# Second layer's q, k and softmax weights turned by VectorE blocks and GpSimd transfers over DRAM, in place of TensorE transposes

## The chip, the cores and the metric

One core of a Trainium2 chip runs the whole program in one launch. The metric is the device time of one execution in microseconds (us). Three runs of the kernel before took 2663.75, 2664.67 and 2666.57 us; their median, 2664.67 us, is the time before. Weights arrive in the order in which the kernel reads them; laying them out so is done ahead of the launch and is not timed.

## The reference

Two layers of a bidirectional encoder over 256 tokens, width 2048, float32. A layer mixes tokens by two attentions in parallel, then applies a gated MLP with a depthwise convolution of width 3. Cut to what matters here:

```python
h = rmsnorm(x, norm_mix[l]) * (1 + sc_a) + sh_a
qa, ka, va, qb, kb, vb, ga, gb = split_cols(h @ w_in[l])
qa = rotary_partial(rmsnorm(qa, qn_a[l]), pos)      # 8 heads of 128; ka: 2 heads
ka = rotary_partial(rmsnorm(ka, kn_a[l]), pos)
ya = window_attention(qa, ka, va, sink_a[l]) @ w_proj_a[l]
qb, kb = rmsnorm(qb, qn_b[l]), rmsnorm(kb, kn_b[l])  # 8 heads of 128 each
yb = neighbourhood_attention(qb, kb, vb, rel_bias_b[l]) @ w_proj_b[l]
x = x + gt_a * ((sigmoid(ga) * ya + sigmoid(gb) * yb) @ w_out[l])
```

Each of the 16 heads of a layer computes softmax(q kT + bias or mask) v over 256 queries and 256 keys.

## The kernel before, in words

**Weights as a stream.** All weight blocks (128x128) of a layer stand in one order (`block_stream`, L90), cut into units of 16 blocks. For a unit, SyncE loads 1 MB into a tile of the pool `raw` (4 tiles, shared with the modulation rows `aw`, L225); ScalarE casts each half to its high part (`hl`, L297), VectorE subtracts to get the low part (L298), and TensorE multiplies both (`feature_block`, L314 to L316, three matmuls a block; `tokens`, L377 to L379, with 512 columns). The pool `hl` holds four halves, so the casts run at most two units ahead. What TensorE multiplies is written out by hand in that order: in the second layer 8 gate rows, nine groups of q, k and v (`QKV_GROUPS`, L33, four units each), the other gate rows, the projection of branch A (`ps<-oA`), the gates of branch B, the projection of branch B, the output, the MLP.

**Work between the units.** At the end of each unit `Stream.tick` (L331) runs `bg.tick` (L258): first what was deferred to the next unit (`bg.defer`, L246), then the jobs, each at a rate of steps a unit. After each group of q or k, `qk_rows` (L539) squares the rows on ScalarE (L547), takes the root as a power on GpSimd (L441), and three units later scales the rows into `qn` on VectorE (L556; one buffer). A unit later `turn` (L576) transposes `qn`, which has tokens on the partitions, head by head on TensorE against an identity matrix (L580), into PSUM, and ScalarE copies it out with the norm's gain (L581). Then `ready` lets heads start. The job `attention` (L842) advances every live head by one step and starts one more; its rate in the second layer is `ATT[1]` = 0.4 steps a unit in the q, k, v and gate stage and `ATT_B[1]` = 0.21 later. `attended(HA)` (L925) steps the job until the 8 heads of branch A are done, before the projection of A; `bg.finish(job)` (L952) does the rest before the projection of B.

**A head.** `head_a` or `head_b` (which loads its bias into `p` by SyncE, L825; `p` has two buffers) splits q and k into high and low parts. `attend` (L602): scores on TensorE (L607), maximum on VectorE (L610), exponential and scaling on ScalarE (L618, L626). In the next step four TensorE transposes turn `p` (L631) into the PSUM tile `tp`, and `split` (L389 ScalarE, L390 VectorE) writes high and low parts into `pT` (one buffer). In the next step TensorE multiplies v by `pT` (L639), and ScalarE and VectorE write `o` (L641, L642).

A tile scheduler puts each engine's instructions into one queue in order, by the program's order and by when it thinks operands are there; an engine never passes a waiting instruction. In the kernel before GpSimd issues no transfer; its work in the second layer's attention is the power at L441. The launch line (L1141) reserves 1024 bytes of each partition for descriptors of dynamic transfers.

Of the kernel before, what the change touches and what calls it, by code (L numbers as in the profile page):

```python
# [9 lines left out]
F32 = mybir.dt.float32  # L10
F32R = mybir.dt.float32r
# [4 lines left out]
P = 128  # L16
# [11 lines left out]
NEG = -1e30  # L28
SCALE = HEAD ** -0.5
GRID_W, NA_KH, NA_KW = 64, 8, 16  # L30


QKV_GROUPS = [1024, 0, 512, 2560, 3584, 1536, 3072, 4096, 2048]  # L33
# [44 lines left out]

H_RATE = [2.7, 1.7]

ATT = [1.288, 0.4]
ATT_B = [0.21, 0.21]

SCORES_3 = (1,)

ADA_ORDER = [[p * KC + k for k in range(KC) for p in ps] for ps in ((0, 1), (2,), (3, 4), (5,))]
ADA_ORDER = [i for part in ADA_ORDER for i in part]
# [47 lines left out]
def encoder(ctx: ExitStack, tc: tile.TileContext, a: dict, out: bass.AP):  # L135
# [16 lines left out]
    sm = pool("sm", 3)  # L152
    mm = pool("mm", 4, space=bass.MemoryType.PSUM)
    ax = pool("ax", 3, space=bass.MemoryType.PSUM)

    ident = const.tile([P, P], F32, name="ident")
    make_identity(nc, ident[:])
# [118 lines left out]
                pass  # L276

    bg = Paced()

    def unit_steps(l, u, by_halves=False):  # L280

# [254 lines left out]
            nc.vector.tensor_tensor(out=z[:], in0=ps[:, :S], in1=self.rbs[:], op=ALU.mult)  # L536
            return z, sh

    def qk_rows(pss, heads, rot, gain, dst, then):  # L539

        cols = 0
        n = heads * HEAD
        ss = sm.tile([P, 8], F32, name="qss", tag="qss")
        for t, ps in enumerate(pss):
            for i in range(heads):
                sq = at.tile([P, HEAD], F32, name="qsq", tag="qsq", bufs=1)
                nc.scalar.activation(  # L547
                    out=sq[:], in_=ps[:, cols + i * HEAD : cols + (i + 1) * HEAD], func=AF.Square,
                    accum_out=ss[:, t * heads + i : t * heads + i + 1],
                )  # L550
        rs = sm.tile([P, 8], F32, name="qrs", tag="qrs")
        rsqrt(rs[:, : 2 * heads], ss[:, : 2 * heads], HEAD, 2 * heads)
        def norm():
            qn = at.tile([P, 2, 4, HEAD], F32, name="qn", tag="qn", bufs=1)
            for t, ps in enumerate(pss):
                nc.vector.tensor_tensor(  # L556
                    out=qn[:, t, :heads],
                    in0=ps[:, cols : cols + n].rearrange("p (h d) -> p h d", d=HEAD),
                    in1=rs[:, t * heads : (t + 1) * heads].unsqueeze(2).broadcast_to([P, heads, HEAD]),
                    op=ALU.mult,  # L560
                )
            if rot is not None:
                x1, x2 = qn[:, :, :heads, :HALF], qn[:, :, :heads, HALF:ROT]
                tab = [rot[:, i].unsqueeze(2).broadcast_to([P, 2, heads, HALF]) for i in range(4)]
                tm = []
                for i in range(2):
                    z = ev.tile([P, S], F32, name=f"rt{i}", tag="z")
                    z = z[:].rearrange("p (i t h d) -> p i t h d", i=2, t=2, h=4)
                    tm += [z[:, 0, :, :heads], z[:, 1, :, :heads]]
                for i, src in enumerate((x1, x2, x2, x1)):  # L570
                    nc.vector.tensor_tensor(out=tm[i], in0=src, in1=tab[i], op=ALU.mult)
                nc.vector.tensor_tensor(out=x1, in0=tm[0], in1=tm[1], op=ALU.subtract)
                nc.vector.tensor_tensor(out=x2, in0=tm[2], in1=tm[3], op=ALU.add)
            bg.defer(lambda: turn(qn))

        def turn(qn):  # L576
            for t in range(2):
                ps = ax.tile([P, 4, P], F32, name="qtp", tag="ax")
                for h in range(heads):
                    nc.tensor.transpose(ps[:, h], qn[:, t, h], ident[:])  # L580
                nc.scalar.activation(  # L581
                    out=dst[:, :, t * P : (t + 1) * P], in_=ps[:, :heads], func=AF.Identity, scale=gain
                )
            then()

        bg.defer(lambda: bg.defer(lambda: bg.defer(norm)))
# [12 lines left out]

        return ((0, 0), (0, 1), (1, 0))[: 2 * len(x) - 1]  # L600

    def attend(q, k, v, p, mask, scale, sink, o):  # L602

        sc = ax.tile([P, 2, S], F32, name="sc", tag="ax")
        for t in range(2):
            for i, j in by(q):
                nc.tensor.matmul(sc[:, t], q[i][:, t * P : (t + 1) * P], k[j], start=i + j == 0, stop=(i, j) == by(q)[-1])  # L607
        m = sm.tile([P, 2], F32, name="m", tag="m")
        for t in range(2):
            nc.vector.tensor_tensor_reduce(  # L610
                out=p[:, t], in0=sc[:, t], in1=mask[:, t], scale=scale, scalar=-3.0e38 if sink is None else sink,
                op0=ALU.add, op1=ALU.max, accum_out=m[:, t : t + 1],
            )
        nm = sm.tile([P, 2], F32, name="nm", tag="nm")
        nc.vector.tensor_scalar(out=nm[:], in0=m[:], scalar1=-1.0, scalar2=None, op0=ALU.mult)
        den = sm.tile([P, 2], F32, name="den", tag="den")
        for t in range(2):
            nc.scalar.activation(out=p[:, t], in_=p[:, t], func=AF.Exp, bias=nm[:, t : t + 1], accum_out=den[:, t : t + 1])  # L618
        if sink is not None:
            es = sm.tile([P, 2], F32, name="es", tag="es")  # L620
            nc.scalar.activation(out=es[:], in_=nm[:], func=AF.Exp, bias=sink)
            nc.vector.tensor_tensor(out=den[:], in0=den[:], in1=es[:], op=ALU.add)
        ri = sm.tile([P, 2], F32, name="ri", tag="ri")
        nc.vector.reciprocal(out=ri[:], in_=den[:])
        for t in range(2):
            nc.scalar.activation(out=p[:, t], in_=p[:, t], func=AF.Copy, scale=ri[:, t : t + 1])  # L626
        yield
        tp = ax.tile([P, 2, S], F32, name="tp", tag="ax")
        for k in range(2):
            for t in range(2):  # L630
                nc.tensor.transpose(tp[:, k, t * P : (t + 1) * P], p[:, t, k * P : (k + 1) * P], ident[:])  # L631
        pT = at.tile([P, 2, 2, S], F32R, name="pT", tag="pT", bufs=1)
        split(pT, tp[:])
        v = v()
        yield
        po = ax.tile([P, 512], F32, name="po", tag="ax")
        for i, j in by(v):
            for b in range(2):
                nc.tensor.matmul(po[:, :S], v[i][:, b], pT[:, j, b], start=i + j + b == 0, stop=i + b == 2)  # L639
        o = o()  # L640
        nc.scalar.copy(o[:, 0], po[:, :S])  # L641
        nc.vector.tensor_tensor(out=o[:, 1], in0=po[:, :S], in1=o[:, 0].bitcast(F32), op=ALU.subtract)  # L642
# [115 lines left out]
    for l in range(L):  # L758
# [41 lines left out]
        def head_a(i):  # L800
            g = i // (HA // GA)
            if i >= 6:
                oA.append(paired(F32R, f"oA{l}_{i}"))
            elif i % 2 == 0:
                o = place(("y0", "y1", "y2")[i // 2], 4, F32R, f"oA{l}_{i}")
                oA.extend((o[:, :2], o[:, 2:]))
            q = in_halves(qTa[:, i], f"qA{l}_{i}", "qh", l in SCORES_3)
            if i % (HA // GA) == 0:
                kvs[0] = in_halves(kTa[:, g], f"kA{l}_{g}", "kh", l in SCORES_3)
            k = kvs[0]  # L810
            yield
            p = at.tile([P, 2, S], F32, name="p", tag="p")

            def v():
                if i % (HA // GA) == 0:
                    kvs[1] = in_halves(packs[0][:, 1:4:2, g * HEAD : (g + 1) * HEAD], f"vA{l}_{g}", "vh", True)
                return kvs[1]

            yield from attend(q, k, v, p, tables[0], SCALE, sink[:, i : i + 1], lambda: oA[i])

        def head_b(hb):
            b, i = packs[1 + hb // 4], hb % 4
            v = b[:, 4:8].rearrange("p (t a) s -> p t (a s)", t=2)
            p = at.tile([P, 2, S], F32, name="p", tag="p")
            nc.sync.dma_start(p[:], a["bias"][l, hb])  # L825
            q = in_halves(b[:, 8 + i], f"qB{l}_{hb}", "qh", l in SCORES_3)
            k = in_halves(b[:, i], f"kB{l}_{hb}", "kh", l in SCORES_3)
            yield
            yield from attend(
                q, k, lambda: in_halves(v[:, :, i * HEAD : (i + 1) * HEAD], f"vB{l}_{hb}", "vh", True), p, p, 1.0, None,  # L830
                lambda: oB_of(hb),
            )

        def oB_of(hb):
# [36 lines left out]
        for pi, (groups, gates) in enumerate(parts):  # L871
            last = pi == len(parts) - 1
            for g, part in enumerate(groups):
# [21 lines left out]
                    for t in range(2):  # L895
                        nc.scalar.copy(rows[:, t, vcol:], pss[t][:, vcol:])
                if g == 0:
                    qk_rows(pss, GA, rots[1], gains[:, 1:2], kTa, turned)
                elif g < 3:
                    qk_rows(pss, 4, rots[0], gains[:, 0:1], dst, turned)  # L900
                elif vcol is None:
                    qk_rows(pss, 4, None, gains[:, 3:4] if g in (3, 6) else gains[:, 2:3], dst, turned)
                else:
                    turned()
                if g == 2:
# [243 lines left out]
```

## Time and profile before

| what | value |
|---|---|
| three runs | 2663.75, 2664.67, 2666.57 us |
| profiled execution | span 2663.2 us from its first to its last instruction (no other time of this execution is listed) |
| TensorE (PE) busy | 2650.9 us, 100% of the span |
| VectorE (DVE) busy | 2102.2 us, 79% |
| ScalarE (ACT) busy | 1412.8 us, 53% |
| GpSimd (POOL) busy | 36.2 us, 1% |
| bytes moved | 700.41 MB in 102039 packets |

Times in the trace count from the start of the span. The second layer's attention lies from 1438 us (the first q or k transpose) to 1802 us (the last gate of branch B); the projection of A begins at 1658 us. A row of the timeline gives the start, the length, engine, line, operation, output and inputs, and in brackets how long the engine had been idle and what it waited for. A row of the groups gives the count, busy time and mean length of one instruction. TensorE's matmuls are pipelined: the length of one (390 ns with 512 columns) is longer than the distance between two (227 ns), so its busy time is no measure of what a removed matmul saves; the distance in the timeline or the chain of work is.

### The profile page before, as it was taken

The page shows a single profiled execution, that of the slowest core. Times are in us where ns is not written, and L with a number is a line of the kernel's source. Part 1 is how long each engine was busy: PE and PEld are TensorE (multiplying, and loading weights), DVE is VectorE, ACT ScalarE, POOL GpSimd, SP SyncE. Part 2 cuts the span into 40 slices and gives each one's busy share as a digit, 9 for nine tenths or more (in the row PEclk, how much of TensorE's full clock was granted, in tenths as well). Part 3 has the DMA queues.
Part 4 walks back from the last instruction along what each step waited for, and adds up shares of the span by engine and source line. Part 5 has one row for each costly group of instructions (what it writes and reads, how often), then busy time and mean ns, then how long its engine had stood idle before and what let it go on. Part 6 is the DMA issues. An engine that isn't in the chain of part 4 may idle for free.

```text
span 2663.2 us, 50845 instructions
## 1 busy us (share of the span) xinstructions
PE 2650.9 (100%) x21256; PEld 2565.7 (96%) x21256; DVE 2102.2 (79%) x2959; ACT 1412.8 (53%) x2284; POOL 36.2 (1%) x25
## 2 busy tenths in 40 slices
PE   9999999999999999999999999999999999999999
PEld 7888899999999999999998889999999999999999
DVE  8898998997987888788976667768888866655664
ACT  5445865456644555355555566554565445544553
POOL 0001100000000000000000000000000000000000
PEclk9999999999999999999999999999999999999999
DMA  9987789885787878788766666666747765555554
GB/s 372 351 327 292 262 300 352 317 320 199 291 294 287 302 288 295 289 294 289 290 217 254 228 229 231 245 252 253 285 173 288 297 256 190 190 194 194 197 191 143
DMA packets 102039, 700.41 MB, mean 263 GB/s; under 512 B 12721, under 2 KB 15025, under 8 KB 17969
## 3 DMA queue, kind: packets, MB, share of 16 engines
q1 hardware_dynamic: 101810, 697.17, 71.4%
q8 instruction: 166, 2.72, 0.4%
q14 instruction: 63, 0.52, 0.1%
HBM read 695.03 MB, written 2.10 MB: 262 GB/s over the span
## 4 chain that ended last, share of the span: by engine, by line
PE 89%; DVE 6%; ACT 1%; issue 1%; DMA 1%; POOL 0%; SPq 0%; DVEq 0%; ACTq 0%
PE ps L314 25%; PE ps L316 25%; PE ps L315 25%; PE ps_t L377 4%; PE ps_t L379 4%; PE ps_t L378 4%; DVE hl L298 2%; DVE aw L226 2%; DMA aw<-in_aw 1%; PE sc L607 1%; PE po L639 1%; ACT hl L297 1%; PE tp L631 1%; POOL qrs L441 0%; PE qtp L580 0%
## 5 line engine op out<-in xcount | busy, mean ns | idle before, releaser
L298 DVE TENSOR_TENSOR hl<-w,hl 128x1024 fp32r<-128x1024 f32 x928 | 1128.3, 1222 | 360.0 <-ACT hl L297 357.6
L297 ACT CAST hl<-w 128x1024 fp32r<-128x1024 f32 x928 | 970.7, 1049 | 748.5 <-PE ps L316 518.1
L314 PE MATMUL ps<-h,hl 128*128 128x256 f32 x3328 | 922.8, 277 | 1.3 <-DVE ya L915 0.6
L315 PE MATMUL ps<-h,hl 128*128 128x256 f32 x3328 | 919.8, 276 | 0.0
L316 PE MATMUL ps<-h,hl 128*128 128x256 f32 x3328 | 919.8, 277 | 0.0
L314 PEld LDWEIGHTS ps<-h,hl 128*128 128x128 f32 x3328 | 624.8, 188 | 2.4 <-DVE ya L915 0.8
L315 PEld LDWEIGHTS ps<-h,hl 128*128 128x128 f32 x3328 | 625.3, 188 | 0.4 <-DVE h L470 0.2
L316 PEld LDWEIGHTS ps<-h,hl 128*128 128x128 f32 x3328 | 624.4, 188 | 0.0
L226 DVE CUSTOM_DVE_ANT_0 aw<-aw,cact,ab 128x2048 f32<-128x2048 f32 x189 | 443.5, 2347 | 48.8 <-DMA aw<-in_aw 47.8
L377 PE MATMUL ps_t<-hl,h 128*128 128x512 f32 x576 | 223.1, 392 | 2.6 <-ACT h L469 2.1
L378 PE MATMUL ps_t<-hl,h 128*128 128x512 f32 x576 | 224.9, 391 | 0.3
L379 PE MATMUL ps_t<-hl,h 128*128 128x512 f32 x576 | 224.3, 390 | 0.0
L994 DVE SCALAR_TENSOR_TENSOR u<-ps,cw,u 128x255 f32<-128x255 f32 x304 | 146.1, 481 | 66.5 <-ACT u L992 62.2
L992 ACT ACTIVATE u<-ps,cw 128x256 f32<-128x256 f32 x152 | 85.9, 565 | 187.9 <-PE ps L316 187.5
L316 PE MATMUL ps<-merged,hl 128*128 128x256 f32 x512 | 141.8, 277 | 0.4 <-DVE hl L298 0.4
L315 PE MATMUL ps<-merged,hl 128*128 128x256 f32 x512 | 141.6, 277 | 0.0
L314 PE MATMUL ps<-merged,hl 128*128 128x256 f32 x512 | 141.6, 277 | 0.0
L315 PE MATMUL ps<-act_o,hl 128*128 128x256 f32 x512 | 141.4, 276 | 0.0
L316 PE MATMUL ps<-act_o,hl 128*128 128x256 f32 x512 | 141.3, 276 | 0.0
L314 PE MATMUL ps<-act_o,hl 128*128 128x256 f32 x512 | 141.2, 276 | 0.0
L377 PEld LDWEIGHTS ps_t<-hl,h 128*128 128x128 f32 x576 | 107.9, 188 | 26.1 <-ACT h L469 3.1
L378 PEld LDWEIGHTS ps_t<-hl,h 128*128 128x128 f32 x576 | 108.1, 188 | 23.7 <-DVE hl L298 1.9
(231 smaller groups left out, 4612.5 us busy)
## 6 DMA issues: line engine op xcount, KB each, us to landing
w<-in_ws SPq DMA_DIRECT2D x463, 1024.0 KB, 4.9
aw<-in_aw SPq DMA_DIRECT2D x189, 1024.0 KB, 6.1
p<-in_bias SPq DMA_DIRECT2D x16, 256.0 KB, 4.2
x<-in_xT SPq DMA_DIRECT2D x4, 512.0 KB, 5.3
aw_o<-in_aw SPq DMA_DIRECT2D x2, 1024.0 KB, 12.3
out<-x SPq DMA_DIRECT2D x16, 128.0 KB, 2.1
w<-in_ws SPq DMA_DIRECT2D x2, 512.0 KB, 11.7
aw_b<-in_aw SPq DMA_DIRECT2D x1, 1024.0 KB, 18.1
```

Of the source, the lines that this page charges most:

```text
L226: nc.vector.tensor_tensor_reduce(out=raw[:], in0=raw[:], in1=cact[:], scale=1.0, scalar=ab[:, i : i + 1], op0=ALU.mult, op1=ALU.add, accum ...
L297: nc.scalar.copy(hl[:, 0], r)
L298: nc.vector.tensor_tensor(out=hl[:, 1], in0=r, in1=hl[:, 0].bitcast(F32), op=ALU.subtract)
L314: nc.tensor.matmul(out, hi, act[0], start=first, stop=False)
L315: nc.tensor.matmul(ps[:, :S], hi, act[1], start=False, stop=False)
L316: nc.tensor.matmul(out, lo, act[0], start=False, stop=last)
L377: nc.tensor.matmul(ps[:], xh, hi, start=kc == kcs[0], stop=False)
L378: nc.tensor.matmul(ps[:], xh, lo, start=False, stop=False)
L379: nc.tensor.matmul(ps[:], xl, hi, start=False, stop=kc == kcs[-1])
L607: nc.tensor.matmul(sc[:, t], q[i][:, t * P : (t + 1) * P], k[j], start=i + j == 0, stop=(i, j) == by(q)[-1])
L992: nc.scalar.activation(out=u, in_=ps, func=AF.Identity, scale=w[:, 1:2], bias=w[:, 3:4])
L994: nc.vector.scalar_tensor_tensor(out=u[:, to], in0=ps[:, of], scalar=w[:, j : j + 1], in1=u[:, to], op0=ALU.mult, op1=ALU.add)
```

## The change

In the second layer (`MOVED = (1,)`) no transpose runs on TensorE. VectorE turns each 32x32 block of the tile in place (`blocks`). Then GpSimd issues eight transfers (`scatter`), each from 32 partitions of one half of the tokens, which put the blocks into their transposed places in a DRAM tile; one contiguous piece is 32 floats, 128 bytes. A transfer of a full q or k group has 512 such pieces, one of `p` or of the first group (2 heads) has 256. A further transfer reads the DRAM tile back: for q and k straight into its place (`dst`), where ScalarE then applies the gain in place; for `p` two transfers, each into a tile of its own (`pk`, pool `ev`, tag `r`, two buffers), from which `split` writes `pT` in two parts. Blocks, scatter, read-back and gain are a unit apart (`in_turn`). A head of the second layer has two more steps, in which it only waits, and the rates rise from 0.4 to 0.5 and from 0.21 to 0.32.

```diff
+BLOCK = 32
-ATT = [1.288, 0.4]
-ATT_B = [0.21, 0.21]
+ATT = [1.288, 0.5]
+ATT_B = [0.21, 0.32]
+MOVED = (1,)
+    dram = pool("dram", 2, space=bass.MemoryType.DRAM)
+    def once(fn):
+        due = [fn]
+        def run():
+            if due:
+                due.pop()()
+        return run
+    def in_turn(*fns):
+        def run(i):
+            fns[i]()
+            if i + 1 < len(fns):
+                bg.defer(lambda: run(i + 1))
+        bg.defer(lambda: run(0))
+    def blocks(t):
+        nc.vector.transpose(out=t, in_=t)
+    def scatter(y, rows):
+        to = y[:].rearrange("(b i) n (t a j) -> t a i n b j", i=BLOCK, t=2, a=P // BLOCK)
+        for t, row in enumerate(rows):
+            src = row.rearrange("p n (b j) -> p n b j", j=BLOCK)
+            for a in range(P // BLOCK):
+                nc.gpsimd.dma_start(to[t, a], src[a * BLOCK : (a + 1) * BLOCK])
...
-    def qk_rows(pss, heads, rot, gain, dst, then):
+    def qk_rows(pss, heads, rot, gain, dst, then, moved=False):
...
         def turn(qn):
+            if moved:
+                for t in range(2):
+                    blocks(qn[:, t, :heads].rearrange("p h d -> p (h d)"))
+                y = dram.tile([P, heads, S], F32, name="qY", tag="qY")
+                def scaled():
+                    nc.scalar.activation(out=dst, in_=dst, func=AF.Identity, scale=gain)
+                    then()
+                in_turn(
+                    lambda: scatter(y, [qn[:, t, :heads] for t in range(2)]), lambda: nc.gpsimd.dma_start(dst, y[:]), scaled
+                )
+                return
...
-    def attend(q, k, v, p, mask, scale, sink, o):
+    def attend(q, k, v, p, mask, scale, sink, o, moved=False):
...
         yield
+        if moved:
+            blocks(p[:].rearrange("p t k -> p (t k)"))
+            y = dram.tile([P, 2, S], F32, name="pY", tag="pY")
+            turned = []
+            def back():
+                for k in range(2):
+                    turned.append(ev.tile([P, S], F32, name="pk", tag="r", bufs=2))
+                    nc.gpsimd.dma_start(turned[k][:], y[:, k])
+            steps = [once(lambda: scatter(y, [p[:, t].rearrange("p (k s) -> p k s", k=2) for t in range(2)])), once(back)]
+            in_turn(*steps)
+            yield
+            yield
+            for step in steps:
+                step()
+            pT = at.tile([P, 2, 2, S], F32R, name="pT", tag="pT", bufs=1)
+            for k in range(2):
+                split(pT[:, :, k], turned[k][:])
+        else:
...
+            split(pT, tp[:])
```

The calls of `attend` and `qk_rows` pass `l in MOVED`.

More of the change, by code (lines that the diff above doesn't have):

```diff
@@ L627, in attend @@
         yield
[L628 to L633, printed above, removed]
+        if moved:
[16 more added lines that the diff above has]
+        else:
+            tp = ax.tile([P, 2, S], F32, name="tp", tag="ax")
+            for k in range(2):
+                for t in range(2):
+                    nc.tensor.transpose(tp[:, k, t * P : (t + 1) * P], p[:, t, k * P : (k + 1) * P], ident[:])
+            pT = at.tile([P, 2, 2, S], F32R, name="pT", tag="pT", bufs=1)
+            split(pT, tp[:])
         v = v()
@@ L817, in v @@
                 return kvs[1]
-            yield from attend(q, k, v, p, tables[0], SCALE, sink[:, i : i + 1], lambda: oA[i])
+            yield from attend(q, k, v, p, tables[0], SCALE, sink[:, i : i + 1], lambda: oA[i], l in MOVED)
         def head_b(hb):
@@ L830, in head_b @@
                 q, k, lambda: in_halves(v[:, :, i * HEAD : (i + 1) * HEAD], f"vB{l}_{hb}", "vh", True), p, p, 1.0, None,
-                lambda: oB_of(hb),
+                lambda: oB_of(hb), l in MOVED,
             )
@@ L897, in encoder @@
                 if g == 0:
-                    qk_rows(pss, GA, rots[1], gains[:, 1:2], kTa, turned)
+                    qk_rows(pss, GA, rots[1], gains[:, 1:2], kTa, turned, l in MOVED)
                 elif g < 3:
-                    qk_rows(pss, 4, rots[0], gains[:, 0:1], dst, turned)
+                    qk_rows(pss, 4, rots[0], gains[:, 0:1], dst, turned, l in MOVED)
                 elif vcol is None:
-                    qk_rows(pss, 4, None, gains[:, 3:4] if g in (3, 6) else gains[:, 2:3], dst, turned)
+                    qk_rows(pss, 4, None, gains[:, 3:4] if g in (3, 6) else gains[:, 2:3], dst, turned, l in MOVED)
                 else:
```

## The prediction

> **What bounds the kernel now.** I read the page's busy times first, then the busy time by stretches, then the chain of work over the second layer's attention, then the timeline around it.
>
> ```profile
> PE 2650.9 (100%) x21256; PEld 2565.7 (96%) x21256; DVE 2102.2 (79%) x2959; ACT 1412.8 (53%) x2284; POOL 36.2 (1%) x25
> ...
> PEclk9999999999999999999999999999999999999999
> ```
>
> TensorE is never idle and its clock is granted in full, so a matmul taken out of its queue is time gained, and every wait that reaches it is time lost. The stretches of the stage that changes (before and after 1647 us, where the last head of branch A must be done):
>
> ```profile
> core 0: us, PE busy (x) PEld busy (x) DVE busy (x) ACT busy (x) POOL busy (x), PEclk, DMA share, GB/s
> 1440.00:1647.00 207.00, 206.94 (x1149) 179.85 (x1148) 142.09 (x221) 126.75 (x279) 9.87 (x6) 1.00 0.63 233
> 1647.00:1802.00 155.00, 155.00 (x1361) 155.00 (x1360) 107.56 (x169) 83.32 (x150) 0.00 (x0) 1.00 0.67 246
> ```
>
> VectorE works 142 of 207 us, ScalarE 127, the 16 DMA engines 63%, GpSimd 10. There is room everywhere but on TensorE. How much lead the others have over it shows in the timeline:
>
> ```profile
> 1433.24 1.05 ACT L297 CAST hl<-w 128x1024 fp32r<-128x1024 f32 x1 [1.67 <-PE ps_t L379]
> 1435.96 1.05 ACT L297 CAST hl<-w 128x1024 fp32r<-128x1024 f32 x1 [1.67 <-PE ps_t L379]
> 1437.04 1.23 DVE L298 TENSOR_TENSOR hl<-w,hl 128x1024 fp32r<-128x1024 f32 x1 [1.50 <-ACT hl L297]
> ```
>
> TensorE uses half a unit in 1435.96 - 1433.24 = 2.72 us, a unit in 5.44. A cast starts when one of four half buffers comes free, so three halves are ready: 3 x 2.72 = 8.2 us, less 1.05 and 1.23 to make the next, leaves a **lead of 5.9 us**. ScalarE or VectorE may stand still that long before TensorE waits.
>
> **The change, part by part: the gain.** 52 transposes of q and k (2 heads x 2, six groups of 4 x 2) and 64 of `p` (16 x 4) go; the built program of the changed kernel has exactly 116 fewer. The chain has their price:
>
> ```profile
> 1438.64 0.44 PE qtp L580 x4
> 1460.92 0.87 PE qtp L580 x8
> ...
> 1518.85 0.44 PE tp L631 x4
> ```
>
> 0.44 / 4 = 0.87 / 8 = 0.11 us each, so 116 x 0.11 = 12.8 us at most; the timeline shows 0.35 us for four where the next matmuls close up (0.09 each):
>
> ```profile
> 1600.78 0.60 PE L631 MATMUL tp<-ident,p 128*128 128x128 f32 x4
> 1601.13 0.94 PE L607 MATMUL sc<-kA,qA 128*128 128x256 f32 x6
> ```
>
> That gives 10.2 us. I take **12 us**.
>
> **VectorE and ScalarE.** Every price is from these rows of the attention's stretch:
>
> ```profile
> L390 DVE TENSOR_TENSOR pT<-tp,pT 128x512 fp32r<-128x512 f32 x16 | 10.9, 682 | 0.1
> L389 ACT CAST pT<-tp 128x512 fp32r<-128x512 f32 x16 | 9.5, 595 | 0.0
> L389 ACT CAST vB<-packB 128x256 fp32r<-128x256 f32 x8 | 3.4, 421 | 0.0
> L390 DVE TENSOR_TENSOR vB<-packB,vB 128x256 fp32r<-128x256 f32 x8 | 3.3, 415 | 0.0
> L581 ACT ACTIVATE packB<-qtp,gains 128x512 f32<-128x512 f32 x8 | 5.1, 687 | 0.0
> ```
>
> No block transpose is in the trace; nearest is 682 ns for 512 columns (one input instead of two may make it half, a slower form double): 28 x 0.68 + 2 x 0.42 = 20 us, 10 to 40. The split of `p` in two costs VectorE 32 x 0.415 - 10.9 = 2.4 us more, ScalarE 32 x 0.421 - 9.5 = 4.0. ScalarE's gain over 1024 columns (some 1.05 us, as the cast of that width) in place of two of 0.69 saves under 3 us. In the first stretch (14 blocks of q and k, 8 of heads, some 15 us) VectorE rises to 157 of 207 us and is still idle a quarter of it; the added work comes in pieces of 0.7 us, inside a lead of 5.9. Cost **0**, hidden behind TensorE's matmuls; were the lead gone, the 20 + 2.4 = 22 us would be paid.
>
> **The transfers.** GpSimd's queue gets 7 x 8 scatters of q and k, 16 x 8 of `p`, 7 + 32 read-backs: 223 transfers; the scatters are 48 x 512 + 8 x 256 + 128 x 256 = 59,392 pieces of 128 bytes. The trace has no transfer of GpSimd's. What it has:
>
> ```profile
> q1 hardware_dynamic: 101810, 697.17, 71.4%
> ...
> out<-x SPq DMA_DIRECT2D x16, 128.0 KB, 2.1
> ...
> ab<-in_ab SPq DMA_DIRECT2D x2, 48.0 KB, 6.2
> ...
> gains<-in_gains SPq DMA_DIRECT2D x2, 2.0 KB, 4.4
> ```
>
> ```profile
> 1435.57 0.33 SPq L225 DMA_DIRECT2D aw<-in_aw  x1
> ```
>
> Below, one transfer costs the queue what SyncE needs to issue one, 0.33 us, and the rest overlaps; above, each waits for the one ahead to land, 6.2 us (`ab`, 128 short rows under load). The nearest row is `out<-x`: also into DRAM, 128 rows, 2.1 us. A scatter of 512 pieces has four times the pieces and half the bytes; I put it between 2.1 and the 4.4 of `gains` (128 rows of 16 bytes), at **3.0 us**; one of 256 pieces, of which the built order lets several be under way, between 0.33 and 2.1, at **1.3**; a read-back at 1.0. [...]
>
> **Who waits.** The scatter starts when VectorE has made the blocks. Two units and the gain's unit later, 16.3 us after them, ScalarE meets the gain; behind it stand the casts of `hl`. With the lead that is 22 us for 8 x 3.0 = 24, a landing of 2.1, the read-back's 1.0 and its 2.1: 29. It is 7 us late by itself. Behind the scatter in GpSimd's queue stands the next group's power (L441), VectorE's `qn` waits for that and the subtractions stand behind `qn`; already now:
>
> ```profile
> DVE qn L556 <- POOL qrs L441: 10.6, 6, 1.8
> ```
>
> It is the same lateness, paid once. For `p`, four units (21.8 us) and the lead stand against 8 x 1.3 + 2.1 + 2 + 2.1 = 16.6: in time, unless a group's scatter is ahead in the queue. From the fourth group on it is, as the built order mixes them. SyncE's load of `p` for a head of branch B must wait until the scatter two heads back has read its buffer, and the weight loads stand behind it. Now it waits for the transposes:
>
> ```profile
> SPq L825 <- PE tp L631: 35.7, 14, 5.2
> ```
>
> Eight scatters land 12.5 us after the blocks, and the built order puts that load some two units (10.9 us) after them: 1.6 us, inside the raw tiles' lead. Cost 0; with a backlog it is not.
>
> **The sum.** As each wait pushes the next, I count GpSimd's queue as a whole up to the last head of branch A, whose turned weights the projection of A needs. In the built order six full groups, the small one and eight heads stand ahead of it: 48 x 3.0 + 8 x 1.3 + 6 x 1.0 + 64 x 1.3 + 16 x 1.0 = 259.6 us, and 9.9 of powers (the stretch's POOL column), and 3 us for landing and split: 272.5 against 207 us. **65.5 us late.** In the second stretch eight heads take 8 x (8 x 1.3 + 2) = 99 of 155 us: nothing. So 2663.2 - 12 + 65.5 = 2716.7 us for the profiled execution's span; the median of the three runs, 2664.67, lies 1.5 above that span: **2718 us**.
>
> **The rivals.**
>
> A. *The transfers are hidden.* If 512 pieces cost 1.8 and 256 cost 0.95 or less (the queue overlaps landings), with 0.6 a read-back, the demand is 86 + 8 + 61 + 13 + 10 = 178 of 204 us, and a lone group takes 14.4 + 4.8 = 19 of 22 us. Then only the gain is left: 2664.7 - 12 = 2653 (2651.9 with 12.8). For it: GpSimd is idle and a third of the DMA time is free. Against it: 59,392 pieces where the whole kernel now has 102,039 packets. It ends on the other side, and decides where the queue's demand falls below the stretch. Chance 0.21. If it misses by as much as it gains, no change: 0.05.
>
> B. *Every scatter waits for the one ahead.* At 4.4 us (`gains`) for 512 and 2.1 (`out<-x`) for 256: 211 + 17 + 6 + 134 + 16 + 10 + 3 = 397, 190 late: 2664.7 - 12 + 190 = 2843. For it: eight transfers to a group, one queue, and a reserve of 1024 bytes for descriptors. Against: landing times under SyncE's 1 MB loads contain the wait behind those in one queue. [...] Chance 0.20.
>
> C. *The pieces crowd the weights.* In the first stretch 48 x 512 + 8 x 256 + 64 x 256 = 43,008 pieces are 2688 on each engine; 37% of 207 us is free, 77 us, so it decides from 28 ns a piece. The q1 row gives 0.714 x 16 x 2663.2 / 101,810 = 0.30 us for a packet of 6.8 KB; by bytes alone 128 take 6 ns. At 50 ns, 134 us: 57 late, 2710. It would show as ScalarE's casts waiting for `w`. Chance 0.10.
>
> D. *VectorE keeps GpSimd out.* If each of the 142 transfers of the first stretch also waited for a subtraction (1.23 us, above): 175 more, 2893. [...] The trace of before has no transfer of GpSimd's and cannot show it.
>
> For D: VectorE is busy two thirds of the stretch. Against: the 10 us that GpSimd's powers took in it show no such delay, 1.6 us each. Chance 0.05.
>
> That the change does not do what it says is excluded by the built program's count of transposes.
>
> **How the numbers follow.** Forecast 2718 us, chance 0.39; A 0.21, no change 0.05, B 0.20, C 0.10, D 0.05. Faster by over 0.2% (below 2659.3): A alone, 0.21. Slower by over 0.2% (above 2670.0): 0.39 + 0.20 + 0.10 + 0.05 = 0.74. 0.2% is about what a measurement of this kernel can tell from no change. The range: below, A's full gain, 2651; above, prices that reach past B's 2843 to D's 2893. It leaves out the bound of 6.2 us a transfer (142 x 6.2 alone is 880 us, far over 207) and the halves of D above 2893.
>
> **What would show it.** Right: `qtp` and `tp` gone from the second layer; TensorE idle between 1440 us and the projection of A by some 60 us, put down to VectorE's `qn` and ScalarE's gain, which wait for GpSimd and its transfers; the stretch after it as long as before less its transposes; a full group's eight scatters holding GpSimd's queue for some 24 us. Wrong: no idle TensorE (A); casts of `hl` waiting for `w` from DRAM (C); a stretch of the first layer or the MLP that changes its length, which no step here touches; a scatter that occupies the queue for over 4 us (B).

## The result and the profile after

The changed kernel takes **2775.59 us** (median of 4 runs, 2774.72 to 2780.65) against 2664.6 us of the kernel before (4 runs, 2663.75 to 2666.57): 1.042 times as long, interval 1.040 to 1.043. The forecast was 2718 us: the sign and the place were right, the loss of 111 us is twice the 53 foreseen. The profiled execution took 2776.42 us, its span is 2774.2.

The page of the changed kernel; the busy times, then TensorE's share, the granted clock in 40 slices of 69.4 us, and GpSimd's DMA queue (packets, MB, share of the DMA engines):

```profile
PE 2666.5 (96%) x21140; PEld 2571.6 (93%) x21140; DVE 2115.8 (76%) x3005; ACT 1409.0 (51%) x2293; POOL 178.7 (6%) x248
...
PE   9999999999999999999997877799999999999999
...
PEclk9999999999999999999998888899999999999999
...
q0 software_dynamic: 8368, 15.22, 2.2%
```

All is as before but for the slices of the second layer's attention: there TensorE idles, and its clock, always full before, is granted at eight tenths. The same stretch of work by windows, first the kernel before, then the changed one (from 1440 us to the first matmul of the projection of A, and on to that of B; the columns are the stretch, its length, the busy time of PE, PEld, DVE, ACT and POOL, the granted clock, the DMA share and GB/s):

```profile
1440.00:1658.00 218.00, 217.94 (x1245) 190.85 (x1244) 149.57 (x235) 133.43 (x292) 9.87 (x6) 1.00 0.63 232
1658.00:1802.30 144.30, 144.30 (x1267) 144.30 (x1266) 100.08 (x154) 76.94 (x136) 0.00 (x0) 1.00 0.68 249
```

```profile
1440.00:1764.50 324.50, 233.51 (x1171) 197.49 (x1170) 161.11 (x269) 132.74 (x300) 108.11 (x156) 0.85 0.57 188
1764.50:1913.80 149.30, 144.89 (x1225) 144.30 (x1225) 105.17 (x166) 79.55 (x143) 39.20 (x65) 0.97 0.74 267
```

The first stretch is 106.5 us longer, the second 5. TensorE stood still for 324.5 + 149.3 - 233.5 - 144.9 = **95.4 us**. Its matmuls were busy for 378.4 us where before they took 362.2 and should have taken about 352 without the transposes (9.9 us, measured below): **26 us** more, at a clock of 0.85. 95.4 + 26.1 - 9.9 = 111.6, the whole difference. The one group of matmuls below shows the slower clock: in the stretch up to 1764 us the mean of one (in ns, behind the comma), before and after:

```profile
L378 PE MATMUL ps_t<-hl,h 128*128 128x512 f32 x223 | 86.9, 390 | 0.0
```

```profile
L413 PE MATMUL ps_t<-hl,h 128*128 128x512 f32 x222 | 93.3, 420 | 43.8 <-DVE hl L333 43.5
```

Who waited for what in the changed kernel from 1416 to 1830 us (total us, times, longest):

```profile
POOL qY L313 <- issue: 129.1, 45, 6.7
...
ACT packB L618 <- DMA packB<-qY: 67.2, 4, 26.0
DVE qn L591 <- POOL qrs L476: 62.4, 6, 21.2
POOL pY L313 <- issue: 60.4, 46, 4.1
...
ACT packA L618 <- DMA packA<-qY: 46.7, 3, 19.1
ACT pT L424 <- DMA pk<-pY: 44.1, 13, 11.9
```

These are the waits the prediction named: ScalarE's gain (L618) for the read-back, VectorE's `qn` for the power in GpSimd's queue. New is the first row: GpSimd itself, with nothing that the view names to wait for, stands 129 us between scatters of q and k. Its timeline over one full group shows how:

```profile
1460.50 0.77 POOL L313 DMA_DIRECT2D qY<-qn  x1 [6.00 <-DVE qn L305]
1463.20 0.75 POOL L313 DMA_DIRECT2D qY<-qn  x1 [1.94 <-issue]
1468.49 0.74 POOL L313 DMA_DIRECT2D qY<-qn  x1 [4.54 <-issue]
...
1484.44 0.74 POOL L313 DMA_DIRECT2D qY<-qn  x1 [1.91 <-issue]
1485.19 1.67 POOL L476 TENSOR_TENSOR qrs<-qss,mhalf 128x8 f32<-128x8 f32 x1
1487.08 0.61 POOL L622 DMA_DIRECT2D packA<-qY  x1 [0.21 <-issue]
```

A scatter of 512 pieces is issued in 0.75 us, and the next one starts 1.9 us after that, or 4.5. What it waits for stands in the trace's records of landings, of which the page gives the median from issue to landing (us, last):

```profile
qY<-qn POOLq DMA_DIRECT2D x48, 64.0 KB, 2.4
```

The first three of these scatters landed at 1462.87, 1468.19 and 1470.87 us; the second, third and fourth start at 1463.20, 1468.49 and 1471.17. In all six full groups each of the seven later scatters starts 0.30 to 0.35 us after the one ahead has landed, whether the wait is 1.9 or 6.7 us. The eight take 1485.18 - 1460.50 = 24.7 us; the six full groups took 24.7 to 28.6. The power for the next group, ready long before, starts right behind the eighth (1485.19). Of scatters of 256 pieces three go out at once, in 2.03 us, and the fourth starts 0.31 us after the first has landed (1428.27, 1428.58); the eight of the first head take 10.2 us.

ScalarE in the same group: its last cast, and the gain.

```profile
1472.46 1.05 ACT L332 CAST hl<-w 128x1024 fp32r<-128x1024 f32 x1 [1.22 <-PE ps_t L414]
1490.82 1.15 ACT L618 ACTIVATE packA<-packA,gains 128x1024 f32<-128x1024 f32 x1 [17.30 <-DMA packA<-qY]
```

It stood 17.3 us in front of the gain, with the casts of `hl` behind it, and TensorE ran dry.

### The profile page after: what moved, and what is told of

Same layout as the page of the kernel before. It is cut to its first block, busy times and chain, and to the rows that moved or that the text cites. A ratio compares the mean times of both kernels' runs of the same rounds, so it can differ in the third digit from the quotient of the medians.

```text
span 2774.2 us, 51127 instructions
## 1 busy us (share of the span) xinstructions
PE 2666.5 (96%) x21140; PEld 2571.6 (93%) x21140; DVE 2115.8 (76%) x3005; ACT 1409.0 (51%) x2293; POOL 178.7 (6%) x248
## 3 DMA queue, kind: packets, MB, share of 16 engines
q0 software_dynamic: 8368, 15.22, 2.2%
## 4 chain that ended last, share of the span: by engine, by line
PE 75%; DVE 7%; issue 7%; DMA 5%; POOL 3%; ACT 2%; SPq 0%; POOLq 0%; DVEq 0%; ACTq 0%
PE ps L349 22%; PE ps L351 22%; PE ps L350 22%; DVE hl L333 3%; DMA aw<-in_aw 3%; PE ps_t L413 2%; PE ps_t L414 2%; PE ps_t L412 2%; DVE aw L230 2%; ACT hl L332 1%; POOL pY L313 1%; POOL qY L313 1%; DMA w<-in_ws 1%; POOL qrs L476 1%; DMA pY<-p 0%
## 5 line engine op out<-in xcount | busy, mean ns | idle before, releaser
L413 PE MATMUL ps_t<-hl,h 128*128 128x512 f32 x576 | 231.7, 403 | 44.0 <-DVE hl L333 43.5
L412 PE MATMUL ps_t<-hl,h 128*128 128x512 f32 x576 | 228.1, 401 | 15.0 <-ACT hl L332 13.0
L414 PE MATMUL ps_t<-hl,h 128*128 128x512 f32 x576 | 229.0, 398 | 0.0
L413 PEld LDWEIGHTS ps_t<-hl,h 128*128 128x128 f32 x576 | 111.2, 193 | 72.9 <-DVE hl L333 49.9
L412 PEld LDWEIGHTS ps_t<-hl,h 128*128 128x128 f32 x576 | 110.9, 193 | 40.5 <-ACT hl L332 14.3
```

The source lines that it names most:

```text
L412: nc.tensor.matmul(ps[:], xh, hi, start=kc == kcs[0], stop=False)
L413: nc.tensor.matmul(ps[:], xh, lo, start=False, stop=False)
L414: nc.tensor.matmul(ps[:], xl, hi, start=False, stop=kc == kcs[-1])
```

## The experiments

Theory R: the reserve for GpSimd's descriptors (1024 bytes) holds one 512-piece transfer or three of 256, so scatters wait for landings. Its rivals are a price by the piece (P), VectorE holding GpSimd out (V), and reasons in the program's order. Intervals are those of the ratio to the kernel before on the same chip.

**A larger reserve.** To make room, the scratch tile of the squares was put into a tile that is dead at that time (`...` stands for the rest of a line).

```
-sq = at.tile([P, HEAD], F32, name="qsq", tag="qsq", bufs=1)
+sq = ev.tile([P, HEAD], F32, name="qsq", tag="sqa", bufs=1)
-nc = _bacc.Bacc(..., dynamic_dma_scratch_size=1024)
+nc = _bacc.Bacc(..., dynamic_dma_scratch_size=1536)
```

> The changed kernel with 1536 instead of 1024 bytes reserved for GpSimd's descriptors; room for it is made by letting the squares' scratch tile (qsq, 512 bytes a partition) share the tile of rbs. Theory R (the reserve holds one 512-piece transfer or three of 256, so each 512-piece scatter waits until the one ahead has landed): two 512-piece scatters fit now, a group's eight take 8 x (0.75 + 1.9) / 2 = 11 to 14 us in place of 26.8, and a group's 11 + 2 + 1 + 2 fits into the 22 us ahead of the gain. Nearly all of the 111 us goes: 2655 to 2685 us. Theory P (the price is by the piece: GpSimd needs the time to make 512 descriptors, or the DMA engines to move 512 pieces): a scatter keeps 2.65 us, the time stays within 10 us of 2776. Theory V (VectorE's instructions hold GpSimd out while it writes descriptors): also 2776.

Measured 2699.61 us, ratio 1.0118 (1.0103 to 1.0133): 32 us over the kernel before on the same chip, so **79 us of the 111 are gone** for 512 bytes. GpSimd's timeline over the same group:

```profile
1459.06 1.51 POOL L313 DMA_DIRECT2D qY<-qn  x2 [6.00 <-DVE qn L305]
1461.73 0.74 POOL L313 DMA_DIRECT2D qY<-qn  x1 [1.17 <-issue]
...
1475.11 0.74 POOL L313 DMA_DIRECT2D qY<-qn  x1 [3.74 <-issue]
```

Two go out at once, as R says, at the same 0.75 us each, and the eight take 16.8 us in place of 24.7. By the records of landings the third starts 0.3 us after the first landed (1461.41), and the last 0.3 us after the sixth (1474.81): two are in flight where there was one. P and V fall as the main cause: pieces, DMA engines and VectorE's work are the same. But 2700 is above R's 2655 to 2685: the reserve is not all. The control, the moved scratch tile alone:

> The changed kernel with only the edit that made room for the larger reserve: qsq shares the tile of rbs, the reserve stays at 1024 bytes. If the reserve did it: 2776 within 5 us. If the shared tile did it: 2700.

2775.7 us (one run): it was the reserve.

**Few pieces.** The eight scatters stay in their places and write whole rows (`m` is half a row); the turn across blocks is left out.

```
-to = y[:].rearrange("(b i) n (t a j) -> t a i n b j", i=BLOCK, t=2, a=P // BLOCK)
+m = y.shape[1] * P
+to = y[:].rearrange("p n s -> p (n s)")
...
-src = row.rearrange("p n (b j) -> p n b j", j=BLOCK)
+src = row.rearrange("p n d -> p (n d)")
...
-nc.gpsimd.dma_start(to[t, a], src[a * BLOCK : (a + 1) * BLOCK])
+rs = slice(a * BLOCK, (a + 1) * BLOCK)
+nc.gpsimd.dma_start(to[rs, t * m : (t + 1) * m], src[rs])
```

> The changed kernel with as many scatters of the same bytes in the same places of the program, but each writes whole rows: 32 pieces of 2 KB (q, k), 1 KB (the softmax weights, the small group) instead of 512 or 256 of 128 bytes. The turn across blocks is left out by that. Theory R: 32 pieces leave many transfers room in the reserve, so each costs the queue only its issue, 0.6 to 0.75 us, and lands hidden: 2652 to 2675 us. Theory P: issue falls with the pieces too, well below 0.6 us, 2652 to 2660. Theory F (every transfer of GpSimd's queue waits for the one ahead whatever its size): scatters keep 2.65 us, 2750 to 2776.

2693.22 us, 1.0098 (1.0081 to 1.0115). No theory had that. The queue's waits between scatters are gone as R says, and F is wrong, yet 26 us over the kernel before remain. One group in VectorE's, GpSimd's and ScalarE's timelines (the lines of this kernel lie two lower):

```profile
1457.88 1.30 DVE L305 STREAM_TRANSPOSE qn<-qn 128x512 f32<-128x512 f32 x2
```

```profile
1458.88 4.00 POOL L315 DMA_DIRECT2D qY<-qn  x8 [5.84 <-DVE qn L305]
1469.22 0.57 POOL L624 DMA_DIRECT2D packA<-qY  x1 [6.35 <-DMA qY<-qn]
```

```profile
1463.86 1.04 ACT L334 CAST hl<-w 128x1024 fp32r<-128x1024 f32 x1
1474.53 1.15 ACT L620 ACTIVATE packA<-packA,gains 128x1024 f32<-128x1024 f32 x1 [9.37 <-DMA packA<-qY]
```

VectorE's blocks were done at 1459.2. From there the rest of the issues took 3.7, the landing 6.3, the read-back with its landing 5.3: 15.3 us to the gain. ScalarE was there after 5.7 us (1464.9). In the built order five casts stand between blocks and gain (seven in the changed kernel), and ScalarE had run three of them already, ahead of a VectorE that had waited for the power and the rotary sums. So this run has few pieces and also a gain that stands one to four casts earlier; the two are not told apart. A distance in casts is one in ScalarE's program and not of time between two engines.

**Each part alone.** `l in MOVED` was taken out at one of the two places.

> The changed kernel with q and k of the second layer turned by TensorE as before; only the softmax weights go through VectorE's blocks and DRAM. Queue: a head's 8 x 1.28 + 2 x 0.56 = 11.4 us in every 13 to 20 us between heads, four units (21.8 us) and the lead ahead of the split. Theory R: hidden, the 64 transposes saved are 7 us: 2656 to 2668. [...]

2683.21 us, 1.0062 (1.0045 to 1.0079): not hidden, 16 to 17 us slower.

> The changed kernel with only q and k moved; the softmax weights are turned by TensorE as before. Queue's total 6 x 26.8 + 10 + 4 + 10 = 185 us of 207, less than the stretch. Theory R with the chain (each full group is late by itself: 26.8 + 2.2 + 1 + 4 = 34 us against 16.3 to the gain and 5.9 of lead, 12 late, six times, and TensorE's clock falls in the waits): 2664.7 - 6 + 72 + some 15 of clock = 2720 to 2760. Theory Q (only the queue's total counts, as the prediction added it): below the stretch, so hidden: 2658 to 2670.

2752.12 us, 1.0314 (1.0294 to 1.0334): 84 us slower, inside R's range; theory Q, the prediction's way of adding, falls: a queue that has work for 185 of 207 us loses 84. The two parts make 17 + 84 = 101 of the 111.

> Reserve of 1536 bytes, and only the softmax weights moved (q and k turned by TensorE); with 1024 bytes that took 2683. Theory R (three 256-piece scatters in flight become five): a head's queue time falls from some 11 to 7 us, 2658 to 2670. If the waits come from the places in the program (the split of p, ScalarE's and VectorE's order, rates): within 5 us of 2683.

**2659.46 us, 0.9975 (0.9966 to 0.9985)**: with the larger reserve the softmax weights' turn is hidden, and the kernel is 0.15 to 0.34% faster than the kernel before. TensorE's longest wait from 1416 to 1830 us is 0.9 us:

```profile
PE sc L655 <- ACT packB L629: 0.9, 1, 0.9
```

How many scatters of 256 pieces go out at once with 1536 bytes shows in the small group of a run further down (q and k alone, two empty steps): five, where it was three.

```profile
1424.62 3.21 POOL L313 DMA_DIRECT2D qY<-qn  x5 [3.65 <-DVE qn L305]
1428.71 0.62 POOL L313 DMA_DIRECT2D qY<-qn  x1 [0.88 <-issue]
```

**The price of the transposes and of VectorE's blocks.** The transposes left out, `dst` and `pT` read from `qn` and `p`; then the same with the blocks.

> The kernel before with the second layer's 116 transposes left out and nothing in their place (q, k and the softmax weights go on unturned, so that part of the computation is left out); ScalarE and VectorE read the same widths from SBUF instead of PSUM. It gives the gain by itself. The prediction's 12 us: 2653. If other engines are late without the transposes too: within 4 us of 2664.6.

2659.95 us beside 2670.22 of the kernel before on that chip, ratio 0.9963 (0.9950 to 0.9975): 9.9 us, between 6.7 and 13.3.

> The last one with VectorE's block transposes put in (28 of 128x512, 2 of 128x256), no transfer; the turn across blocks is left out. If VectorE's 20 us hide behind TensorE, as predicted: within 2 us of the one without turns, some 2653. If VectorE is the bound in places: up to 20 us more, 2673.

2656.38 us, 0.9950 (0.9936 to 0.9963): the intervals of the two meet. The blocks cost nothing that can be measured. In the changed kernel they are 16 of `p` at 706 ns and 12 of `qn` at 694, 19.4 us in all:

```profile
L305 DVE STREAM_TRANSPOSE p<-p 128x512 f32<-128x512 f32 x16 | 11.3, 706 | 1.6 <-ACT p L674 1.6
L305 DVE STREAM_TRANSPOSE qn<-qn 128x512 f32<-128x512 f32 x12 | 8.1, 694 | 0.0
```

**The rates.** In the kernel before, `ATT = [1.288, 0.5]` and `ATT_B = [0.21, 0.32]` alone.

> The kernel before with only the change's two rates (0.5 for 0.4 and 0.32 for 0.21), all transposes on TensorE. If the rates matter by themselves: 2658 to 2661, and the gain with only the weights moved (2659.5) isn't the transposes'. If they don't: within 2 us of the kernel before, and the 5 us are the 64 transposes'.

2665.12 us, 1.0000 (0.9991 to 1.0009): nothing. So the rates by themselves do not make the gain with the weights moved; what is left for it is the transposes.

**Another queue.** `nc.gpsimd.dma_start` in `scatter` became `nc.sync` or `nc.scalar`.

> The changed kernel with its 184 scatters issued by SyncE instead of GpSimd; the read-backs stay on GpSimd. [...] Theory R: the scatters no longer wait for space; eight take 2.6 us of SyncE's time if pieces don't count there; SyncE waits for VectorE's blocks and its weight loads stand behind, but four units lie loaded. Only the gain is left if the read-back lands in time: 2650 to 2662. Theory P (512 pieces of 128 bytes cost the DMA engines their time, from whichever queue): still over 2720. If SyncE makes descriptors at a price by the piece, the weight loads are late: casts wait for w, 2680 to 2760.

> The same with the scatters issued by ScalarE. Eight issues of 0.33 us or less are 2.6 us of ScalarE's time a group or head, 22 x 2.6 = 57 us of its time in 365, where it is idle 40%, in pieces inside the lead of 5.9 us: 2650 to 2662 by theory R. If an issue of 512 pieces takes ScalarE over 0.75 us, its casts are late at every group: 2670 to 2720.

2726.49 us (1.0211, 1.0197 to 1.0225) and 2727.53 us (1.0216, 1.0199 to 1.0233): half the loss, and R's 2650 to 2662 fails for both. SyncE's time lies where P had it (over 2720) and where a price by the piece at SyncE had it (2680 to 2760); ScalarE's lies above its 2670 to 2720. An issue costs SyncE 0.63 us in the median (ns, least, median and most, in the view of the tile), not 0.33:

```profile
L313 SPq DMA_DIRECT2D qY<-qn x56: 570/628/2086, 1433.5 to 1669.2; - x56
```

From ScalarE, casts stand behind the issues:

```profile
ACT hl L332 <- issue: 29.5, 9, 6.8
```

The sign of late weight loads, casts that wait for `w`, is not among ScalarE's waits in the run from SyncE. What else makes up the 56 us of these two was not taken apart; whether P holds in these two queues stays open.

**More distance to the gain.** Two empty steps between read-back and gain, first with the small reserve, then with the large, then with the large and q and k alone.

```
-lambda: nc.gpsimd.dma_start(dst, y[:]), scaled
+lambda: nc.gpsimd.dma_start(dst, y[:]), lambda: None, lambda: None, scaled
```

> The changed kernel, reserve of 1024 bytes, with the gain (and what follows from it) two units later: two empty steps between read-back and gain. Theory R: a full group's eight scatters take 26.8 us of the queue, TensorE makes the next group's rows in 4 x 5.44 = 21.8 us, so room ahead of the gain helps only until the queue is behind by itself: less than half of the 111 us goes, 2720 to 2765. Theory L (only the gain stands too early; the queue has the time): 2655 to 2690.

> Reserve of 1536 bytes and the gain two units later, together. With the larger reserve alone 2700 us were left, and ScalarE still waited 70 us in seven places for read-backs. Theory L2 (what is left is the landing of scatter and read-back, some 5 us each under the weights' loads, against a gain that ScalarE reaches earlier than three units after VectorE's blocks): the seven waits go, 2658 to 2680. If what is left is the softmax weights' transfers or the clock: within 8 us of 2700.

> The last one with the softmax weights turned by TensorE as before and the rates of before; only q and k are moved. If q and k are hidden by room and reserve: half the gain of the kernel without turns is left, 2658 to 2664. If the transfers still cost: over 2672.

2784.35 us (1.0441, 1.0426 to 1.0457), 2701.55 us (1.0131, 1.0116 to 1.0146) and 2697.14 us (1.0117, 1.0102 to 1.0132). The first two gained nothing over the same versions without the edit (1.0419 and 1.0118); the third, with q and k alone, was not hidden either. That spoke against the distance, wrongly. In ScalarE's built order the gain of each group stood behind the same number of casts of `hl` as without the two steps: 498, 510, 518 and 525 casts for the first four, in both. The order in which the program is written is not the one in which it is built, and the edit had moved none of these gains. So the gain was pinned behind what is written ahead of it:

```
-nc.scalar.activation(out=dst, in_=dst, func=AF.Identity, scale=gain)
+tc.keep_in_program_order(nc.scalar.activation(out=dst, in_=dst, func=AF.Identity, scale=gain))
```

Now it stands at casts 506, 514, 522, 530.

> Reserve of 1536 bytes, the gain two units later and pinned in ScalarE's order behind the casts written ahead of it: 11 to 13 casts of hl now stand between the blocks of a group and its gain instead of 7 to 9. Theory S (the rest of the loss is that ScalarE, whose casts run ahead of VectorE, reaches the gain 6 to 7 us after the blocks, while scatter, landing, read-back and landing take 15 and more): four casts are 10.9 us, the waits of 7 to 11 us go, 2655 to 2668. If the rest lies elsewhere (transfers, softmax weights, clock): within 8 us of 2701.

2686.48 us, 1.0079 (1.0066 to 1.0091): by the ratios 10 and 14 us better than the two versions with the large reserve and no distance (1.0118 and 1.0131), between the two ranges. Of ScalarE's seven waits for read-backs one is left; VectorE's softmax now waits 25.6 us for scatters of `p`, before 16.7 (1416 to 1730 us):

```profile
DVE p L660 <- DMA pY<-p: 25.6, 5, 8.5
...
ACT packB L619 <- DMA packB<-qY: 10.1, 1, 10.1
```

> The same distance with the reserve of 1024 bytes. Theory R and S together: a group's scatters hold the queue 26.8 us where TensorE needs 21.8 for the next group, so distance alone can't hide it: 2710 to 2750. If distance alone were the cause: 2655 to 2675.

2774.23 us, 1.0416 (1.0400 to 1.0432): distance without reserve is worth nothing, and R and S had given it too much. The section on the prediction says why.

> Reserve of 1536 bytes, gain pinned two units later, only q and k moved; the softmax weights are turned by TensorE, rates of before. Without the distance it took 2697. If what is left with everything moved is the meeting of both kinds of scatters in one queue: q and k alone are hidden, the 52 transposes saved are some 5 us, 2658 to 2664. If q and k cost by themselves still (queue of 20 us and more a group, landings): 2672 to 2685.

**2667.25 us, 1.0009 (1.0000 to 1.0018)**: with reserve and distance q and k alone are hidden, except that the some 5 us that their transposes should win are missing. The softmax weights alone are hidden with the reserve. So the 21 us that the version with everything moved still loses arise only where both are moved. That they meet in GpSimd's queue is likely and not shown by a run of its own: VectorE's 25.6 us of waits for scatters of `p`, above, are missing from the trace of the softmax weights alone.

**The clock.** No transfer, only a ScalarE that is late: each gain of the second layer 12 times over.

```
-nc.scalar.activation(out=dst[:, :, t * P : (t + 1) * P], ...)
+for _ in range(12 if busy else 1):
+    nc.scalar.activation(out=dst[:, :, t * P : (t + 1) * P], ...)
```

> The kernel before (transposes by TensorE, no transfer of GpSimd's) in which ScalarE does each gain of the second layer 12 times over, 15 us more a full group in one piece. TensorE then waits about 15.2 - 5.9 = 9.3 us a full group, some 60 us in all: 2725. Theory C1 (the clock falls because TensorE stood idle): the granted clock falls below 0.95 in the slices of the stalls as in the changed kernel, and the time is some 10 us longer still. Theory C2 (it falls because of the transfers): it stays at 1.00.

2710.79 us (one run), 46 us over the kernel before and less than the 60 and more that were expected. TensorE's longest wait, and windows with the clock in the last column but two:

```profile
PE ps_t L377 <- ACT hl L297: 17.4, 3, 8.6
```

```profile
1470.00:1500.00 30.00, 25.17 (x108) 20.14 (x108) 14.56 (x20) 24.72 (x51) 1.68 (x1) 0.94 0.50 185
1500.00:1530.00 30.00, 25.50 (x108) 20.20 (x106) 15.56 (x20) 24.04 (x47) 1.64 (x1) 0.89 0.50 176
1530.00:1560.00 30.00, 21.37 (x91) 16.95 (x90) 16.07 (x25) 23.90 (x53) 0.35 (x1) 0.83 0.48 174
1560.00:1590.00 30.00, 30.00 (x154) 25.48 (x153) 17.12 (x32) 21.38 (x46) 1.29 (x1) 1.00 0.48 176
```

Where TensorE idles 4.5 to 8.6 of 30 us, the clock is 0.83 to 0.94 with no transfer in GpSimd's queue; where it doesn't, 1.00. By the pages TensorE was busy 2667.2 us for 2650.9 of the kernel before: of the 46 us of this run, 16 are slower matmuls and 30 standing still. The other way round, the softmax weights alone with the large reserve have GpSimd's transfers, no idle TensorE and a full clock:

```profile
1650.00:1700.00 50.00, 50.00 (x439) 50.00 (x438) 41.73 (x87) 31.25 (x64) 25.31 (x42) 1.00 0.84 293
```

It is the standing still and not the transfers: C1. After how long a wait the clock falls, none of these rows tells.

## Why the prediction was right and wrong

- **The gain of 12 us:** right, 6.7 to 13.3 measured.
- **VectorE and ScalarE at 0:** right. The blocks took 19.4 us for 28 (forecast 682 ns each, measured 694 and 706), hidden behind the matmuls.
- **The prices of the transfers:** right in sum, in part by luck, as each was put between two rows that have nothing to do with the reserve. A full group's eight took 26.8 us on average, 3.35 each for 3.0; eight of 256 pieces 10.2 us in the first head, 1.28 for 1.3; the read-back's issue 0.6 for 1.0. A lone group was forecast to reach its gain 29 us after the blocks; measured 1490.8 - 1460.6 = 30.2.
- **Why they cost that:** this was not in the forecast but in rival B. Every 512-piece scatter of a full group did wait for the one ahead, at a smaller price than its 4.4: from issue to issue 2.60 us at the least (1614.02 to 1616.62) and 3.35 on average. Those of 256 pieces did not wait one by one, and cost 1.28 for its 2.1. The larger reserve shows that the wait was for room, and the landings show how much there was: one 512-piece transfer in flight at 1024 bytes, two at 1536, and three of 256 pieces at 1024.
- **The step that failed:** "It is the same lateness, paid once", and with it the sum of GpSimd's queue as a whole, which takes for granted that the queue always has something to do. From the first scatter (1424.8 us) to the read-back of the last head of A (1749.0) pass 324.2 us. In them the queue's own work and its standing between scatters are 103.6 + 129.1 + 24.6 = 257 us, for 269.5 forecast (272.5 without the last landing). The other **67 us** it waited for work, 31 of them for blocks and 10 for the squares' sums:

```profile
POOL qY L313 <- DVE qn L305: 16.1, 4, 6.0
POOL pY L313 <- DVE p L305: 15.1, 2, 13.3
POOL qrs L476 <- DVE qss L475: 9.9, 1, 9.9
```

  For the blocks are made from the power that stands behind the scatters in the same queue. The chain of waits of the changed kernel goes round in this loop, one group in each turn (start, length):

```profile
1452.01 2.50 POOL qrs L476
1454.53 1.29 DVE qn L591 x2
1459.34 1.30 DVE qn L305 x2
...
1482.54 1.89 issue
1485.19 1.68 POOL qrs L476
...
1522.23 1.67 POOL qrs L476
```

  Power, norm, blocks, eight scatters, next power: 1485.2 - 1452.0 = 33.2 and then 37.0 us, where TensorE makes a group's rows in 4 x 5.44 = 21.8. From the fourth full group on scatters of `p` stand in the queue as well. The lateness is paid anew with each group: VectorE waits for the power six times, 62.4 us in all. Distance ahead of the gain is not in this loop, and so it gave nothing at the small reserve. There ScalarE's waits for read-backs fell from 113.9 us in seven places to 28.2 in two, but VectorE's for the power stayed (1416 to 1830 us):

```profile
DVE qn L591 <- POOL qrs L476: 53.4, 7, 18.6
...
ACT packB L619 <- DMA packB<-qY: 28.2, 2, 17.1
```

  With q and k alone the loss is 84 us although the queue has fewer than 207 us of work.
- **The distance of 16.3 us and the lead of 5.9 on top:** too long. In the changed kernel ScalarE reached the gain 1473.5 - 1460.6 = 12.9 us after the blocks, with few pieces 5.7: its lead over VectorE had been used up already. Four to eight casts more were worth 10 to 14 us once the reserve was larger.
- **The clock:** left out of the forecast without a reason; in TensorE's account it is 26 us of slower matmuls.
- **Only the softmax weights, in time:** wrong at the small reserve (16 to 17 us), right at the larger.
- **The second stretch, as long as before less its transposes:** some 9 us wrong. It is 5 us longer, where 42 fewer transposes (1267 - 1225 matmuls) should have taken off some 4; TensorE stood 4.4 us in it. **SyncE's bias load at 0:** VectorE waited 13.9 us for it in three places; not tried by itself.
- **Rival A** held for no version with everything moved. **Rival C:** GpSimd's packets took 2.2% of the DMA engines' time, and a tenth of the pieces (184 x 32 = 5,888 for 59,392) gained 5 us more than room for one more scatter did, though with the gain a few casts earlier. **Rival D:** an issue of 512 pieces takes 0.74 to 0.78 us beside VectorE's work, no 1.23 more.

Open stay the last 21 us with everything moved, of which it is shown only that they need both parts, and the 56 us of the scatters from SyncE and ScalarE.

## What to carry to other kernels

Before summing a queue, look for a loop: if what feeds the queue stands behind it in the same queue, each turn costs its whole length, and the sum of the queue's work says too little. The price of GpSimd's transfers of many small pieces was here set by the room for their descriptors (512 bytes more took 79 of the 111 us away); look for issues a landing apart with nothing else to wait for. And after an edit that gives an instruction more distance, look in the built order whether it moved at all.

## What the runs showed of the hardware

- 512 bytes more of reserve let a second 512-piece transfer go out at once; the group of eight fell from 24.7 to 16.8 us.
- In six full groups of the changed kernel each later 512-piece scatter started 0.30 to 0.35 us after the one ahead had landed.
- Waits cost TensorE more than their length: 26 us of slower matmuls beside 95 us of standing still, and 16 beside 30 where only ScalarE was late.
- 59,392 pieces from GpSimd were 5,888 packets (8,368 with the read-backs' 2,480); the same pieces from ScalarE's queue were 62,336 packets in the next row, and an issue of 512 pieces took SyncE 0.63 us in the median, where that of a load in the kernel before took 0.33.

```profile
q10 hardware_dynamic: 62336, 7.61, 1.9%
q0 software_dynamic: 2480, 7.60, 0.8%
```
